# Two mixers' block inverses issued in step, a held-back order for small products, and low-rank products of split parts

## The chip, the cores and the metric

One core of one Trainium2 chip runs the whole kernel. The metric is device microseconds of one execution, the median over the runs shown. TensorE is PE in the rows, its weight loads are PEld, VectorE is DVE, ScalarE is ACT, GpSimd is POOL, SyncE (which issues most transfers) is SP.

## The reference

One layer of a hybrid encoder, 512 tokens of width 2048, all in fp32:

```
y  = RMSNorm(x) @ W_in                      # 59 column blocks of 128 in the kernel
h  = x + concat[GDN(y_gdn), RWKV7(y_rwkv)] @ W_out
h += CrossAttn(RMSNorm(h), RMSNorm(mem))    # 4 heads, 256 memory tokens
h += SquaredReLU-MLP(RMSNorm(h))
out = RMSNorm(h)
```

GDN is the gated delta rule (8 heads of 128), in chunks: with the decays `G`, `gamma = exp(G_i - G_j)` for `i >= j` and 0 elsewhere, and `M = strict_lower(kb k^T * gamma)`, it solves `(M + I) [U W] = rhs` and then scans over the chunks. RWKV-7 (16 heads of 64) is a token recurrence that the kernel also writes as chunks with a triangular inverse. Its decay and its in-context rate come from two products of rank 64: `tanh(w_lo) @ w2` and `a_lo @ a2`.

## The kernel before

The program has two parts. The second (from `vp`, the values of the cross attention, to the end of the MLP) is untouched. The first holds the input projection, both mixers and two products of the cross attention's weights, and is written by a small planner.

**The big stream.** `projections` issues, for each of 59 column blocks, 48 matmuls of 128x512 into `py`: each fp32 weight is split into a high and a low part in float32r (`whi`, `wlo`), and `xhi`, `xlo` likewise, and three products of parts stand for one fp32 product. After the 59 blocks come 16 blocks `kp` and then 32 pieces `kq` of the same kind.

**The mixers.** `rwkv(j)`, j = 0 to 7, does two RWKV heads at a time, `gdn(h)`, h = 0 to 7, one GDN head. Each eats some of the seven `py` blocks of its turn through four row buffers `ybuf`. Their products are small and mostly in plain fp32: 64x64 and 64x128 ones that use a quarter or a half of the array, and 128x64 and 128x128 ones that use all of it. Names as the rows show them: `pW`, `pA` are the two low-rank products of a turn (64 rows deep, 512 wide, on the lower and the upper half of the array). `ri..` and `gj..` are the products of the two levels that put the 16x16 inverses together (`inverse_levels` for GDN, the loop over `l` in `rwkv`); `gi..y`, `gi..z` finish a GDN inverse; `pu`, `pwt` apply the RWKV inverse. `rs` are the steps of the RWKV scan (128x64, 14 of them in a turn), `gs` those of the GDN scan (128x128, ten), each waiting for a VectorE step in between. `gn`, `pn`, `gon`, `pvr` are sums for norms, from `sumh`, `suml`.

**The 16x16 inverses.** `inverse_blocks` writes the triangular matrices to DRAM, reads the diagonal blocks back, solves them on GpSimd in 15 steps of a multiply and an add, and brings them back by DRAM (`bg16T`, `bg16U` for RWKV). For GDN the matrix is made from `E = exp(min(G_i - G_j, mask))`, which `mbias` makes zero on one side; GpSimd multiplies it by the constant `sneg` into `Es`, minus one strictly on the other side, and VectorE multiplies that with `pkk`.

**The planner.** Every mixer, the loader of weights and the big stream are generators that yield operations one at a time. `run` keeps the next operation of each, asks `start` when its engine and its operands would be free (from costs in `cost`, `CROSS` = 150 ns between engines), issues the one that could start first, and so fixes the order on every engine. `after(...)` holds a generator until an event, such as ("gi", h), the GDN head's diagonal inverses. For PE the key is

```
t = start(c[3])
key = (t + (0 if c[3][0] == "PE" else 150 * c[1]), c[1])
```

A RWKV turn is chained to the end of the levels of the one before; `gdn(h + 1)` is chained to the very end of `gdn(h)`. `kq` waits for "gated", the end of the last GDN head.

Of the kernel before, what the change touches and what calls it, by code (L numbers as in the profile page):

```python
# [17 lines left out]
P = 128  # L18
T = 512
# [8 lines left out]
for _n, _w in (("ident", 128), ("ones", 128), ("mA", 128),  # L28
               ("lv64", 2 * 64), ("cen", 64), ("sneg", 128), ("mbias", 128),
               ("rst64", 512)):  # L30
    CST[_n] = (_off, _w)
    _off += _w
# [13 lines left out]
def constants():  # L46
    c = np.zeros((P, NCST), np.float32)

    def put(name, a):
        o, w = CST[name]  # L50
        c[:, o:o + w] = a

    i = np.arange(P)
    put("ident", np.eye(P))
    put("ones", 1.0)
    j = np.arange(64)
    st = (j[:, None] < j[None, :]).astype(np.float32)
    inc = (j[:, None] <= j[None, :]).astype(np.float32)
    put("mA", np.tile(np.concatenate([st, inc], 1), (2, 1)))

    def level(n, s):
        a = np.arange(n)
        blk = a[:, None] // (2 * s) == a[None, :] // (2 * s)
        return (blk & (a[:, None] % (2 * s) >= s) & (a[None, :] % (2 * s) < s)).astype(np.float32)

    put("lv64", np.concatenate([np.tile(level(64, 16 << l), (2, 1)) for l in range(2)], 1))
    put("cen", np.tile(np.eye(64) - 1.0 / 64, (2, 1)))
    put("sneg", -(i[:, None] < i[None, :]).astype(np.float32))
    put("mbias", np.where(i[:, None] <= i[None, :], 1e30, -1e30))
    put("rst64", np.tile((np.arange(512) % 64 != 0).astype(np.float32), (P, 1)))  # L70
    return c


def build(tc, I, out):
# [109 lines left out]
    def cost(op):  # L184
        eng, nm, _, a, k, out, ins, _ = op
        n = out.free_size()
        if eng == "PE":
            l = ins[0]
            if l.dtype == F32R:
                return n * 0.417 + (13.3 if state["shape"] is None else 120.0)  # L190
            sh = (l.partition_size(), l.free_size())
            sw = 0 if state["shape"] == sh or sh == (128, 128) else 100
            if nm == "transpose":
                return sw + (110 if sh[0] > 64 else 40)
            if sh == (64, 64):
                return sw + (32 if op[5].tensor.name[:2] in ("ri", "pa", "pv", "pu", "pw", "pk", "gj") else 59)
            return sw + (115 if sh[0] < 128 and n == 128 else 2 * max(n * 0.84, 114))
# [15 lines left out]

    def start(op):
        eng, out = op[0], where(op[5])
        t, out_ = clock[eng], out
        for b, log in [(where(i), landed) for i in op[6]] + [(out, landed), (out, seen)]:
            x, by = log.get(b, (0.0, eng))
            if log is landed and b is out_ and eng == "SP" and by == "DMA":
                continue  # L220
            t = max(t, x + op[7][0] + (0.0 if by == eng else CROSS))
        return t
# [296 lines left out]
    def projections():  # L519
# [4 lines left out]
        for n in range(2, NIN):  # L524
            if n == NSQ[3] + 3:
                yield after("macc")
                pt = psb("pms", "mm", 2)
                mc = ybuf[macc[0]]
                yield TE.matmul(pt[:, 0:M], ones, mc[:, 0:M], start=True, stop=False)
                yield TE.matmul(pt[:, 0:M], ones, mc[:, M:2 * M], start=False, stop=True)  # L530
                chain(memnorm(pt, mc[:, M:2 * M]), 1)
            if n >= 4:
                yield after("py", n - 2)
            pt = psb(f"py{n}", "mm", 2)
            yield from gemm_([pt], xhi, xlo, 2 * n, left="x" if n == NIN - 1 else None)
            chain(evict(n, pt), 0)
# [20 lines left out]
        for i in range(2 * KD):  # L557
# [4 lines left out]
            if i == 0:  # L562
                yield after("gated")
            pts = [psb(f"kq{n}_{g}_{hh}", t, 2) for hh, t in enumerate(("mm", "mg"))]
# [45 lines left out]

    wa = pq.tile([P, T], F32, name="wa")
    sgh, sgl, sst = (pq.tile([P, T], F32R, name=n) for n in ("sgh", "sgl", "sst"))
# [3 lines left out]
    def rows():  # L616
# [9 lines left out]
        for c in range(4):  # L626
            yield DV.memset(rs128[g8, c * P:c * P + 1], 0.0)
        yield after("derived")
        yield from shiftmix(0, 0, wa)
        yield AC.activation(wa[0:64, :], wa[0:64, :], AF.Tanh)  # L630
        sg1, y2 = tl("gAq"), tl("gkt")
        yield from shiftmix(1, 1, sg1)
# [80 lines left out]

    def inverse_blocks(nm, store, m, tags, temps, ready, out, moved=False):

# [13 lines left out]
        for j in range(15):  # L729
# [3 lines left out]
                                   in1=Td[:, j:j + 1, 0:j + 1].broadcast_to([np_, w, j + 1]), op=ALU.mult)  # L733
            yield GS.tensor_tensor(out=Td[:, j + 1:16, 0:j + 1], in0=Td[:, j + 1:16, 0:j + 1], in1=t, op=ALU.add)
        Ud = D
# [18 lines left out]
    def inverse_levels(nm, Tm, Tt, NT, tags, mx, big):  # L754
# [4 lines left out]
        for l in range(2):  # L759
# [15 lines left out]
            rr = slice(0, P) if l == 0 else hA  # L775
            yield DV.tensor_tensor(out=Tm[rr, 0:2], in0=Tm[rr, 0:2], in1=d[rr, 4:6], op=ALU.add)
            yield DV.tensor_tensor(out=Tm[rr, 2:4], in0=Tm[rr, 2:4], in1=o[rr, 0:2], op=ALU.add)
            if l == 0:
                yield DV.tensor_tensor(out=Tt, in0=Tt, in1=d[:, 0:4], op=ALU.add)
                continue  # L780
            for r in (1, 0):
                w = slice(r * 64, r * 64 + 64)
                for c, h in ((slice(0, 2), HALF[r]), (slice(2, 4), HALF[1 - r])):
                    yield DV.tensor_tensor(out=big[HALF[r], c, w], in0=Tt[h, c], in1=d[h, c], op=ALU.add)


    def rwkv(j):
# [7 lines left out]
        pW, pA = psb(f"pW{j}"), psb(f"pA{j}")  # L795
        yield TE.matmul(pW, lw[0:64, :], wa[0:64, :], start=True, stop=True)
        yield TE.matmul(pA, lw[64:128, :], wa[64:128, :], start=True, stop=True)
        tw = short()
# [113 lines left out]
        for r in range(3):  # L912
            yield SL.dma_start(lg[r * 32:r * 32 + 32, P:2 * P], I["g2b"][:, js])
        yield after("ri", j)
        Tt = inv[1]
        Tm = inv[0]
# [38 lines left out]

        lgs = tile_of(pm, [P, 3 * P], F32R, "lgs", f"lgs{j}", 1)
        yield AC.copy(lgs[0:96, 0:2 * P], lg[0:96, :])
# [48 lines left out]
    def gdn(h):  # L1006
# [31 lines left out]
        yield after("zeros")  # L1038
        E, B = tl("gE"), tl("gqd")
        yield SL.dma_start(E, Rd[h:h + 1, :].broadcast_to([P, T]))  # L1040
# [10 lines left out]
        yield AC.activation(E, E, AF.Exp)  # L1051
        Es = tl("gEs")
        yield GS.tensor_tensor(out=c3(Es), in0=c3(E), in1=K("sneg").unsqueeze(1).broadcast_to([P, 4, P]), op=ALU.mult)
        kn = yield from normed(k_, None, "gkn", 0)
# [3 lines left out]
        for c in range(4):  # L1058
            cs = slice(c * P, (c + 1) * P)
            yield TE.matmul(pkk[:, cs], kn[:, cs], kb[:, cs], start=True, stop=True)  # L1060
        NTm = Es
        yield DV.tensor_tensor(out=NTm, in0=pkk, in1=Es, op=ALU.mult)

        def store(full):
# [4 lines left out]
        chain(inverse_blocks(f"gi{h}", store, 8, ("gkn", "gk", "gqn"), lambda: (tl("sgi"), tl("sgj", 240)),  # L1069
                             after("gq", h), inv, True), 1, ("gi", h))  # L1070
        q_ = yield from conv(1, 0, "gq")
# [26 lines left out]
        zt = gsh()  # L1098
        yield AC.activation(zt, z, AF.Tanh, scale=0.5)
        zs = tl("gz")  # L1100
        yield DV.scalar_tensor_tensor(out=zs, in0=zt, scalar=1.0, in1=z, op0=ALU.add, op1=ALU.mult)
        yfree.append(ys.pop(base + 3))
        yield after("gi", h)
        Tm, Tt = inv
        N3 = c3(NTm)
# [6 lines left out]
        Y = tl("gkn")  # L1112
        yield DV.tensor_copy(Y[hB, 0:256], p4[hB, 0:256])
        p5 = psb(f"gi{h}z", "mg")
# [3 lines left out]
        yield DV.tensor_copy(TtG[hA, :, 64:128], p5[hA, 0:256].rearrange("p (c t) -> p c t", t=64))  # L1118
        vns, Ss = tl("gE"), tl("gEG")
        for c in range(4):  # L1120
            cs = slice(c * P, (c + 1) * P)
            r1 = vb[:, cs]
            if c > 0:
                p1 = psb(f"gs1_{h}_{c}", "scg", 1)
                yield TE.matmul(p1[:, 0:P], wd[:, cs], Ss[:, cs], start=True, stop=True)
                r1 = short(P, "sg")
                yield DV.tensor_tensor(out=r1, in0=vb[:, cs], in1=p1[:, 0:P], op=ALU.subtract)
# [19 lines left out]
        o = tl("gkt")  # L1147
        yield AC.copy(o, po)
        sq = gsh()
        yield AC.activation(sq, o, AF.Square)  # L1150
# [5 lines left out]
        yield SL.dma_start(mixd[h], o)  # L1156
        if h < 7:
            chain(gdn(h + 1), 3)
        else:
            events.add(("gated",))  # L1160
# [870 lines left out]
```

## Time and profile before

| | us |
|---|---|
| runs before: median of 3 (lowest, highest) | 2897.46 (2896.79, 2902.83) |
| the profiled execution | 2898.35 |
| its span, first to last instruction | 2896.6 |
| PE busy in the span | 2870.5 |
| mean granted TensorE clock | 0.999 |

The profile is of one execution. Its span leaves out what lies around the program, 1.75 us. A matmul's row gives its start and a modelled end; since matmuls overlap, what a matmul costs is read from start to start. A plain fp32 matmul leaves two records, one of float32r one, a transpose one.

### The profile page before, as it was taken

How to read it: one execution, taken by the hardware profiler on the slowest of the kernel's cores; microseconds unless marked ns; L12 is line 12 of the kernel's file. 1: busy time of each engine (PE TensorE's matmuls, PEld its weight loads, DVE VectorE, ACT ScalarE, POOL GpSimd, SP SyncE). 2: the span in 40 equal slices, each digit the busy share in tenths (PEclk: the TensorE clock that was granted, in tenths of full speed). 3: DMA queues.
4: the chain of work that ended last, by engine and by line, in shares of the span. 5: the costliest groups of instructions: out<-in, count | busy, mean ns of one | idle time of the engine just before them, and what ended most of it. 6: DMA issues, size and time to landing. Idle time of an engine off the chain costs nothing.

```text
span 2896.6 us, 48156 instructions
## 1 busy us (share of the span) xinstructions
PE 2870.5 (99%) x18458; PEld 2408.6 (83%) x18458; DVE 2223.9 (77%) x3379; ACT 1561.9 (54%) x2256; POOL 310.2 (11%) x704
## 2 busy tenths in 40 slices
PE   9999999999999999999999999999999999999998
PEld 7787787887877888889888888888888878888887
DVE  7676676676676767769866898888998897878776
ACT  7544554554546555664455555555555655454444
POOL 0302213113113000001111100010010000000000
PEclk9999999999999999999999999999999999999999
DMA  5333333424334579797788767788777988776765
GB/s 193 100 89 85 99 90 86 105 69 100 105 98 137 159 243 298 267 308 199 205 218 209 195 194 219 229 234 248 214 206 207 288 261 278 221 261 209 255 191 178
DMA packets 304503, 546.64 MB, mean 189 GB/s; under 512 B 97224, under 2 KB 178380, under 8 KB 303248
## 3 DMA queue, kind: packets, MB, share of 16 engines
q1 hardware_dynamic: 245264, 449.17, 49.3%
q0 software_dynamic: 35840, 67.12, 11.6%
q10 hardware_dynamic: 23168, 27.27, 2.6%
q8 instruction: 145, 2.38, 0.3%
q14 instruction: 86, 0.70, 0.1%
HBM read 479.10 MB, written 131.48 MB: 211 GB/s over the span
## 4 chain that ended last, share of the span: by engine, by line
PE 92%; DVE 3%; DMA 2%; POOL 1%; issue 1%; ACT 1%; SPq 0%; ACTq 0%; POOLq 0%; DVEq 0%
PE py L228 20%; PE upx L1319 8%; PE upx L1321 4%; PE upy L1319 4%; PE dx L1786 4%; PE dx L1785 4%; PE dx L1788 4%; PE vp L122 3%; PE kq L228 3%; PE sc L122 3%; PE at L122 3%; PE kp L228 3%; PE vo L122 3%; PE upy L1321 2%; PE upz L1319 2%; PE opx L1319 2%
## 5 line engine op out<-in xcount | busy, mean ns | idle before, releaser
L130 ACT CAST whi<-ub 128x1024 fp32r<-128x1024 f32 x290 | 304.5, 1052 | 274.1 <-PE dy L1786 59.0
L131 DVE TENSOR_TENSOR wlo<-ub,whi 128x1024 fp32r<-128x1024 f32 x290 | 352.6, 1220 | 60.5 <-ACT whi L130 55.1
L228 PE MATMUL py<-xhi,whi 128*128 128x512 f32 x928 | 371.0, 400 | 6.3 <-ACT xhi L228 6.3
L228 PE MATMUL py<-xlo,whi 128*128 128x512 f32 x928 | 372.1, 401 | 0.0
L228 PE MATMUL py<-xhi,wlo 128*128 128x512 f32 x912 | 370.9, 407 | 0.0
L228 ACT CAST whi<-wraw 128x1024 fp32r<-128x1024 f32 (+1 forms) x180 | 187.3, 1041 | 260.9 <-PE py L228 162.1
L130 ACT CAST whi<-ua 128x1024 fp32r<-128x1024 f32 x205 | 215.5, 1051 | 191.3 <-PE dx L1786 62.3
L131 DVE TENSOR_TENSOR wlo<-ua,whi 128x1024 fp32r<-128x1024 f32 x205 | 249.7, 1220 | 52.6 <-ACT whi L130 51.8
L228 DVE TENSOR_TENSOR wlo<-wraw,whi 128x1024 fp32r<-128x1024 f32 (+1 forms) x178 | 223.2, 1254 | 70.5 <-ACT whi L228 68.1
L1319 PE MATMUL upx<-cb,whi 128*128 128x512 f32 x992 | 249.8, 394 | 0.7 <-DVE sl L1277 0.7
L228 PEld LDWEIGHTS py<-xhi,whi 128*128 128x128 f32 x928 | 175.3, 189 | 40.6 <-ACT xhi L228 6.6
L228 PEld LDWEIGHTS py<-xlo,whi 128*128 128x128 f32 x928 | 174.9, 189 | 38.3 <-DVE xlo L228 1.0
L1319 PEld LDWEIGHTS upx<-cb,whi 128*128 128x128 f32 x992 | 178.5, 189 | 33.0 <-DVE sl L1277 0.9
L228 PEld LDWEIGHTS py<-xhi,wlo 128*128 128x128 f32 x912 | 172.4, 189 | 32.7 <-issue 1.0
L1785 PE MATMUL dx<-whi,dh 128*128 128x512 f32 x480 | 186.7, 389 | 0.0
L1786 PE MATMUL dx<-whi,dl 128*128 128x512 f32 x480 | 186.7, 389 | 0.0
L1321 PEld LDWEIGHTS upx<-cb,wlo 128*128 128x128 f32 x992 | 135.3, 190 | 9.7
L1321 PE MATMUL upx<-cb,wlo 128*128 128x256 f32 x992 | 138.3, 282 | 0.0
L131 DVE TENSOR_TENSOR wlo<-wr,whi 128x1024 fp32r<-128x1024 f32 x80 | 97.7, 1223 | 43.5 <-ACT whi L130 42.4
L1788 PE MATMUL dx<-wlo,dh 128*128 128x512 f32 x480 | 128.6, 389 | 0.0
L228 ACT ACT_TABLE_LOAD x86 | 110.3, 1283 | 26.2 <-DVE suml_gn L228 11.6
L1319 PE MATMUL upy<-cb,whi 128*128 128x512 f32 x496 | 124.3, 392 | 0.0
(898 smaller groups left out, 6676.2 us busy)
## 6 DMA issues: line engine op xcount, KB each, us to landing
ws<-in_w_dn POOLq DMA_DIRECT2D x128, 512.0 KB, 7.2
wraw<-in_w_in SPq DMA_DIRECT2D x116, 512.0 KB, 3.8
ua<-in_w_dn SPq DMA_DIRECT2D x108, 512.0 KB, 4.5
ub<-in_w_up SPq DMA_DIRECT2D x71, 512.0 KB, 6.3
ua<-in_w_up SPq DMA_DIRECT2D x56, 512.0 KB, 4.7
ub<-in_w_dn SPq DMA_DIRECT2D x52, 512.0 KB, 4.7
sl<-cd SPq DMA_DIRECT2D x104, 256.0 KB, 5.0
ub<-ws SPq DMA_DIRECT2D x52, 512.0 KB, 4.2
```

Of the source, the lines that this page charges most:

```text
L122: PE.matmul(o, l, r, start=start, stop=stop)
L130: tie(S.copy(hi, src))
L131: V.tensor_tensor(out=lo, in0=src, in1=hi.bitcast(F32), op=ALU.subtract)
L228: f(*a, **k)
L1319: PE.matmul(pt, hi[:, k * P:k * P + P], parts[k], start=start and k == 0, stop=False, skip_group_check=True)
L1321: PE.matmul(pt[:, HA], lo[:, k * P:k * P + P], parts[k][:, HA], start=False, stop=k == 7, skip_group_check=True)
L1785: PE.matmul(pts[t], uh[:, x], hi[:, w], start=start and z == 0 and q == 0, stop=False, skip_group_check=True)
L1786: PE.matmul(pts[t], ul[:, x], hi[:, w], start=False, stop=False, skip_group_check=True)
L1788: PE.matmul(pts[t], uh[:, x], lo[:, w], start=False, stop=z == 1 and q == 3, skip_group_check=True)
```

## The change

Eight edits, all in the first part:

1. `sneg` and `Es` go. The GDN matrix is `pkk * E` with the other sign; the sign is taken back by `subtract` in place of `add` in `inverse_blocks`, `inverse_levels`, and by -1 in the copy `Y` (now a tensor_scalar).
2. `cost` charges a float32r matmul that follows a plain fp32 one of fewer than 128 rows 210 ns for the change of shape, not 120, and `run` adds `HOLD` = 150 ns to the start of a plain fp32 matmul that would follow a float32r one.
3. For j, h < 6 the RWKV levels wait for the GDN head to be as far ("gr"), and the GDN levels for the RWKV turn ("rr").
4. `wa` is split once into `wah`, `wal`, each turn's weights `lw` into `lws`; `pW` and `pA` become three float32r products each.
5. `gdn(h + 1)` is chained to the end of the head's inverse. Its tiles that were shared with the scan get buffers of their own (`gvn`, `gSs`, `gr`, `gqe`), and it waits for "gs" (the scan's products) and "ge" (the end) of the head before, ahead of q and of z.
6. `kq` waits for "solved", the last head's inverse, not for "gated".
7. The sums of the memory's norm wait for one `py` more.
8. A tile is renamed (`lgs`).

```
-    CROSS = 150.0
+    CROSS, HOLD = 150.0, 150.0
...
-                return n * 0.417 + (13.3 if state["shape"] is None else 120.0)
+                return n * 0.417 + (13.3 if state["shape"] is None else 120.0 if state["shape"][0] == P else 210.0)
...
                 t = start(c[3])
+                if c[3][0] == "PE" and state["shape"] is None and shape_of(c[3]) is not None:
+                    t = max(t, start(c[3], 0.0) + HOLD)
...
-                yield after("gated")
+                yield after("solved")
...
-    wa = pq.tile([P, T], F32, name="wa")
+    wah, wal = (pq.tile([P, T], F32R, name=n) for n in ("wah", "wal"))
...
+        yield from split_(wa, wah, wal)
...
-        yield TE.matmul(pW, lw[0:64, :], wa[0:64, :], start=True, stop=True)
-        yield TE.matmul(pA, lw[64:128, :], wa[64:128, :], start=True, stop=True)
+        lws = tile_of(pm, [P, 2 * P], F32R, "lws", f"lws{j}", 1)
+        yield from split_(lw, lws[:, 0:P], lws[:, P:2 * P])
+        for n, (l, r) in enumerate(((0, wah), (0, wal), (P, wah))):
+            for p_, h in ((pW, hA), (pA, hB)):
+                yield TE.matmul(p_, lws[h, l:l + P], r[h, :], start=n == 0, stop=n == 2)
...
         yield after("ri", j)
+        events.add(("rr", j))
+        if j < 6:
+            yield after("gr", j)
...
-        Es = tl("gEs")
-        yield GS.tensor_tensor(out=c3(Es), in0=c3(E), in1=K("sneg").unsqueeze(1).broadcast_to([P, 4, P]), op=ALU.mult)
...
-        NTm = Es
-        yield DV.tensor_tensor(out=NTm, in0=pkk, in1=Es, op=ALU.mult)
+        NTm = tl("gEs")
+        yield DV.tensor_tensor(out=NTm, in0=pkk, in1=E, op=ALU.mult)
...
+        if h:
+            yield after("gs", h - 1)
         q_ = yield from conv(1, 0, "gq")
...
+        if h:
+            yield after("ge", h - 1)
         zs = tl("gz")
...
         yield after("gi", h)
+        events.add(("gr", h))
+        if h < 6:
+            yield after("rr", h)
...
-        yield DV.tensor_copy(Y[hB, 0:256], p4[hB, 0:256])
+        yield DV.tensor_scalar(out=Y[hB, 0:256], in0=p4[hB, 0:256], scalar1=-1.0, scalar2=None, op0=ALU.mult)
...
-        vns, Ss = tl("gE"), tl("gEG")
+        if h < 7:
+            chain(gdn(h + 1), 3)
+        else:
+            events.add(("solved",))
+        vns, Ss = tl("gvn"), tl("gSs")
...
-        if h < 7:
-            chain(gdn(h + 1), 3)
-        else:
+        events.add(("ge", h))
+        if h == 7:
             events.add(("gated",))
```

What these edits do to the order shows in three places. The first is PE at the levels of turn 3 (`ri3` RWKV, `gj3` GDN, `po` and `pov` outputs of RWKV, `rs_3` its scan). Before:

```order
L228 MATMUL py_5417<-xhi_376,whi_5320 128x512
L228 MATMUL py_5417<-xlo_377,whi_5320 128x512
L228 MATMUL rs_3_6_5491<-BK_4862,BTz 128x64
L228 MATMUL py_5417<-xhi_376,wlo_5321 128x512
L228 MATMUL gj3u_5500<-gkn_5478,gqn_5390 64x64 x2
L228 MATMUL gj3t_5501<-gkn_5478,gqn_5390 64x64 x2
L228 MATMUL gj3u_5500<-gkn_5478,gqn_5390 64x64 x2
L228 MATMUL rs_3_7_5510<-Qs_4919,WTz 128x64
L228 MATMUL gj3t_5501<-gkn_5478,gqn_5390 64x64 x2
L228 MATMUL gj3u_5500<-gqn_5390,gkn_5478 64x64 x8
L228 MATMUL py_5417<-xhi_387,whi_5419 128x512
```

Now:

```order
L231 MATMUL ri3w_5420<-r_5044,GB_4737 64x64
L231 MATMUL gj3u_5433<-gkn_5341,gqn_5277 64x64 x2
L231 MATMUL gj3t_5434<-gkn_5341,gqn_5277 64x64 x2
L231 MATMUL gj3u_5433<-gkn_5341,gqn_5277 64x64 x2
L231 MATMUL gj3t_5434<-gkn_5341,gqn_5277 64x64 x2
L231 MATMUL gj3u_5433<-gqn_5277,gkn_5341 64x64 x8
L231 MATMUL py_5304<-xhi_377,wlo_5255 128x512
L231 MATMUL py_5304<-xhi_388,whi_5306 128x512
L231 MATMUL py_5304<-xlo_389,whi_5306 128x512
L231 MATMUL ri3u_5467<-E_289_5045,k_5418 64x64 x2
L231 MATMUL pov_5468<-GA_4736,BK_4964 64x64
```

The GDN levels stood in the RWKV scan and were cut by its steps; now they stand between the RWKV levels, with no `py` between the two. The second place is PE at the low-rank products of turn 3 (`pW`, `pA`) and what is around them. Before:

```order
L228 MATMUL py_3978<-xhi_398,whi_3980 128x512
L228 MATMUL rs_2_1_4100<-BK_3631,BTz 128x64
L228 MATMUL pW_4050<-wa,lw_4048 128x512
L228 MATMUL pA_4051<-wa,lw_4048 128x512
L228 MATMUL rs_2_2_4111<-Qs_3688,WTz 128x64
L228 MATMUL py_3978<-xlo_399,whi_3980 128x512
L228 MATMUL pqk_4118<-gqn_4068,gkn_3777 128x128 x4
```

Now:

```order
L231 MATMUL gi2y<-gk_3981,gEs_3808 64x64 x3
L231 MATMUL pW_4301<-wah,lws_4303 128x512
L231 MATMUL pA_4302<-wah,lws_4303 128x512
L231 MATMUL rs_2_2_4359<-BK_3695,BTz 128x64
L231 MATMUL gi2z<-TtG,gkn_4356 64x64 x4
L231 MATMUL pW_4301<-wal,lws_4303 128x512
L231 MATMUL rs_2_3_4371<-Qs_3761,WTz 128x64
L231 MATMUL pA_4302<-wal,lws_4303 128x512
L231 MATMUL gs_2_0_4376<-gv_4031,TtG 128x128
L231 MATMUL pW_4301<-wah,lws_4303 128x512
L231 MATMUL rs_2_3_4385<-BK_3695,BTz 128x64
L231 MATMUL pA_4302<-wah,lws_4303 128x512
```

The two products became six, cut apart by steps of both scans, which now run side by side. The third place is GpSimd after the RWKV inverses of turn 2 (`sr`) and ahead of those of GDN head 2 (`sgi`). Before:

```order
L228 TENSOR_TENSOR sr_3474<-sr_3474,sr_3475 64x15
L228 COPY sr_3474<-sr_3474 64x256
L228 TENSOR_TENSOR gEs_3598<-gE_3460,cst 128x512
L228 MEMSET sgi_3863 32x256
L228 MEMSET sgi_3863 32x16
```

Now:

```order
L231 TENSOR_TENSOR sr_3512<-sr_3512,sr_3513 64x15
L231 COPY sr_3512<-sr_3512 64x256
L231 MEMSET sgi_3824 32x256
L231 MEMSET sgi_3824 32x16
L231 TENSOR_TENSOR sgj_3825<-sgi_3824 32x15
```

The mask's multiply is gone in all eight heads; the rest of GpSimd's list is the same.

## Rows read from the trace of the kernel before

**Rows 1.** The page: the chain that ended last, shares of the span by engine.

```profile
PE 92%; DVE 3%; DMA 2%; POOL 1%; issue 1%; ACT 1%; SPq 0%; ACTq 0%; POOLq 0%; DVEq 0%
```

**Rows 2.** Busy us by stretch, split where `vp` begins: PE, PEld, DVE, ACT, POOL, clock.

```profile
0.00:1125.00 1125.00, 1110.91 (x9403) 903.82 (x9404) 776.49 (x1407) 617.75 (x881) 202.08 (x547) 1.00 0.43 123
1125.00:2896.60 1771.60, 1759.56 (x9057) 1504.79 (x9055) 1447.43 (x1973) 944.14 (x1376) 108.08 (x157) 1.00 0.77 231
```

**Rows 3.** Who PE waited for, 0 to 1125 us: total, times, longest.

```profile
PE gn L228 <- DVE suml_gn L228: 2.6, 3, 0.9
PE ri6x L228 <- DMA r<-bg16T: 1.6, 2, 1.4
PE pu L228 <- ACT whi L228: 1.3, 1, 1.3
PE ri0t L228 <- DMA E<-bg16U: 0.6, 1, 0.6
```

**Rows 4.** Timeline of PE around one 64x64 stretch (`pu`, `pwt`): start, us.

```profile
358.69 0.39 PE L228 MATMUL py<-xhi,wlo 128*128 128x512 f32 x1
359.00 0.27 PE L228 MATMUL pu<-tA,E 64*64 64x64 f32 x2
...
359.11 0.22 PE L228 MATMUL pu<-tA,E 64*64 64x64 f32 x2
...
359.17 0.23 PE L228 MATMUL pu<-tA,E 64*64 64x64 f32 x2
...
360.10 0.50 PE L228 MATMUL py<-xhi,whi 128*128 128x512 f32 x1
360.44 0.40 PE L228 MATMUL py<-xlo,whi 128*128 128x512 f32 x1
```

**Rows 5.** Timeline of PE around one lone scan step.

```profile
365.02 0.40 PE L228 MATMUL py<-xlo,whi 128*128 128x512 f32 x1
365.26 0.33 PE L228 MATMUL rs<-BK,BTz 128*128 128x64 f32 x2
365.40 0.48 PE L228 MATMUL py<-xhi,wlo 128*128 128x512 f32 x1
365.72 0.39 PE L228 MATMUL py<-xhi,whi 128*128 128x512 f32 x1
```

**Rows 6.** Timeline of PE around the low-rank products of turn 3.

```profile
367.54 0.33 PE L228 MATMUL rs<-BK,BTz 128*128 128x64 f32 x2
367.80 0.69 PE L228 MATMUL pW<-wa,lw 64*128 64x512 f32 x1
367.81 0.69 PE L228 MATMUL pA<-wa,lw 64*128 64x512 f32 x1
...
368.93 0.43 PE L228 MATMUL rs<-Qs,WTz 128*128 128x64 f32 x2
369.17 0.48 PE L228 MATMUL py<-xlo,whi 128*128 128x512 f32 x1
369.49 0.50 PE L228 MATMUL pqk<-gqn,gkn 128*128 128x128 f32 x3
```

**Rows 7.** The mask on GpSimd, a weight split on VectorE, the wait on PE.

```profile
L228 DVE TENSOR_TENSOR wlo<-wraw,whi x178: 684/1225/2756, 10.0 to 1120.5; 128x1024 fp32r<-128x1024 f32 x176, 128x512 fp32r<-128x512 f32 x2
...
223.48 2.75 DVE L228 TENSOR_TENSOR wlo<-wraw,whi 128x1024 fp32r<-128x1024 f32 x1 [1.80 <-ACT whi L228]
...
223.84 1.30 POOL L228 TENSOR_TENSOR gEs<-gE,cst 128x512 f32<-128x512 f32 x1
...
226.88 0.50 PE L228 MATMUL gn<-suml_gn,onesr 128*128 128x512 f32 x1 [0.88 <-DVE suml_gn L228]
```

**Rows 8.** Timeline of the end of one GDN inverse.

```profile
394.88 0.67 PE L228 MATMUL gi2y<-gk,gEs 64*64 64x64 f32 x8
...
396.74 0.43 DVE L228 COPY gkn<-gi2y 64x256 f32<-64x256 f32 x1
...
397.52 0.68 PE L228 MATMUL gi2z<-TtG,gkn 64*64 64x64 f32 x8
```

More of the change, by code (lines that the diff above doesn't have):

```diff
@@ L28 @@
 for _n, _w in (("ident", 128), ("ones", 128), ("mA", 128),
-               ("lv64", 2 * 64), ("cen", 64), ("sneg", 128), ("mbias", 128),
+               ("lv64", 2 * 64), ("cen", 64), ("mbias", 128),
                ("rst64", 512)):
@@ L67, in constants @@
     put("cen", np.tile(np.eye(64) - 1.0 / 64, (2, 1)))
-    put("sneg", -(i[:, None] < i[None, :]).astype(np.float32))
     put("mbias", np.where(i[:, None] <= i[None, :], 1e30, -1e30))
@@ L212, in cost, with shape_of, start @@
         return 100.0
-    def start(op):
+    def shape_of(op):
+        l = op[6][0]
+        return None if l.dtype == F32R else (l.partition_size(), l.free_size())
+    def start(op, t=None):
         eng, out = op[0], where(op[5])
-        t, out_ = clock[eng], out
+        t, out_ = clock[eng] if t is None else t, out
         for b, log in [(where(i), landed) for i in op[6]] + [(out, landed), (out, seen)]:
@@ L526, in projections @@
                 yield after("macc")
+                yield after("py", n - 1)
                 pt = psb("pms", "mm", 2)
@@ L628, in rows @@
         yield after("derived")
+        wa = tl("gqd")
         yield from shiftmix(0, 0, wa)
         yield AC.activation(wa[0:64, :], wa[0:64, :], AF.Tanh)
+        yield from split_(wa, wah, wal)
         sg1, y2 = tl("gAq"), tl("gkt")
@@ L712, in views, with inverse_blocks @@
         return full, blk
-    def inverse_blocks(nm, store, m, tags, temps, ready, out, moved=False):
+    def inverse_blocks(nm, store, m, tags, temps, ready, out, moved=False, op=ALU.add):
         np_ = 4 * m
@@ L733, in inverse_blocks @@
                                    in1=Td[:, j:j + 1, 0:j + 1].broadcast_to([np_, w, j + 1]), op=ALU.mult)
-            yield GS.tensor_tensor(out=Td[:, j + 1:16, 0:j + 1], in0=Td[:, j + 1:16, 0:j + 1], in1=t, op=ALU.add)
+            yield GS.tensor_tensor(out=Td[:, j + 1:16, 0:j + 1], in0=Td[:, j + 1:16, 0:j + 1], in1=t, op=op)
         Ud = D
@@ L775, in inverse_levels @@
             rr = slice(0, P) if l == 0 else hA
-            yield DV.tensor_tensor(out=Tm[rr, 0:2], in0=Tm[rr, 0:2], in1=d[rr, 4:6], op=ALU.add)
-            yield DV.tensor_tensor(out=Tm[rr, 2:4], in0=Tm[rr, 2:4], in1=o[rr, 0:2], op=ALU.add)
+            yield DV.tensor_tensor(out=Tm[rr, 0:2], in0=Tm[rr, 0:2], in1=d[rr, 4:6], op=ALU.subtract)
+            yield DV.tensor_tensor(out=Tm[rr, 2:4], in0=Tm[rr, 2:4], in1=o[rr, 0:2], op=ALU.subtract)
             if l == 0:
-                yield DV.tensor_tensor(out=Tt, in0=Tt, in1=d[:, 0:4], op=ALU.add)
+                yield DV.tensor_tensor(out=Tt, in0=Tt, in1=d[:, 0:4], op=ALU.subtract)
                 continue
@@ L783, in inverse_levels @@
                 for c, h in ((slice(0, 2), HALF[r]), (slice(2, 4), HALF[1 - r])):
-                    yield DV.tensor_tensor(out=big[HALF[r], c, w], in0=Tt[h, c], in1=d[h, c], op=ALU.add)
+                    yield DV.tensor_tensor(out=big[HALF[r], c, w], in0=Tt[h, c], in1=d[h, c], op=ALU.subtract)
     def rwkv(j):
@@ L954, in rwkv @@
             chain(rwkv(j + 1), 3)
-        lgs = tile_of(pm, [P, 3 * P], F32R, "lgs", f"lgs{j}", 1)
+        lgs = tile_of(pm, [P, 3 * P], F32R, "lgs", f"lg_s{j}", 1)
         yield AC.copy(lgs[0:96, 0:2 * P], lg[0:96, :])
@@ L1038, in gdn @@
         yield after("zeros")
-        E, B = tl("gE"), tl("gqd")
+        E, B = tl("gE"), tl(("gqd", "gqe")[h % 2])
         yield SL.dma_start(E, Rd[h:h + 1, :].broadcast_to([P, T]))
@@ L1069, in gdn @@
         chain(inverse_blocks(f"gi{h}", store, 8, ("gkn", "gk", "gqn"), lambda: (tl("sgi"), tl("sgj", 240)),
-                             after("gq", h), inv, True), 1, ("gi", h))
+                             after("gq", h), inv, True, ALU.subtract), 1, ("gi", h))
+        if h:
+            yield after("gs", h - 1)
         q_ = yield from conv(1, 0, "gq")
@@ L1125, in gdn @@
                 yield TE.matmul(p1[:, 0:P], wd[:, cs], Ss[:, cs], start=True, stop=True)
-                r1 = short(P, "sg")
+                r1 = tl("gr", P, 2)
                 yield DV.tensor_tensor(out=r1, in0=vb[:, cs], in1=p1[:, 0:P], op=ALU.subtract)
@@ L1146, in gdn @@
                 yield TE.matmul(po[:, cs], Ss[:, cs], qd[:, cs], start=False, stop=True)
-        o = tl("gkt")
+        events.add(("gs", h))
+        o = tl("gSs")
         yield AC.copy(o, po)
-        sq = gsh()
+        sq = tl("gvn")
         yield AC.activation(sq, o, AF.Square)
```

## The prediction

> **What bounds the kernel now.** The chain that ended last is PE for 92% of the span [rows 1]; read it first, since it says that an edit pays only if it takes time from PE or lets PE wait less. [...] The second part, 1771.6 us, is untouched, and I carry it over. Third, who PE waited for in the first part [rows 3]: the four longest, leaving the start aside, are 6.1 us in all. So the mixers are hidden beside the big stream, and what they cost is the time their own small products hold PE. That is read from start to start around a stretch of them [rows 4 to 6]; a big float32r matmul takes 0.23 to 0.24 us so measured (365.02 to 365.26).
>
> Times are summed against the profiled execution, 2898.35 us (span 2896.6 and 1.75 around it). The median of the runs shown is 0.9 us lower, and I subtract the sum from that median. A measurement of this kernel tells about 0.2%, 5.8 us, from no change.
>
> **The change, part by part.**
>
> *Levels in step, held-back products (edits 2, 3, 5).* No product is added; they are regrouped. A stretch of 64x64 products costs more than its products: from the last `py` before `pu` to the second one after it are 1.75 us (358.69 to 360.44), of which two big matmuls are 0.47; the thirty products go in fifteen rounds of 0.06 (359.11 to 359.17), 0.9; so entering and leaving cost 0.4 [rows 4]. In the built order PE goes from full-size products into 64x64 ones 111 times before and 96 times after. 15 x 0.4 = 6.0 us less. I use the whole price, since a stretch that vanishes takes both ends with it.
>
> The scan steps: before, 69 `rs` and 80 `gs` stood alone between big matmuls; now 43 and 29 do, and 50 times an `rs` stands right before a `gs`. A lone `rs` costs 0.70 - 0.47 = 0.23 [rows 5]. What a pair saves no row shows. Bounds: nothing, and half a lone `rs`, 0.12, as it streams half the columns that a `gs` does: 0 to 6.0 us. An `rs` behind `pA` moved the next start by 0.24 [rows 6], as a lone one does, so I stay near nothing: 1.5.
>
> *Low-rank products (edit 4).* Before, a pair takes 1.13 us (367.80 to 368.93), and `rs` ahead of it is 0.12 longer than a lone one's 0.14 (0.26 against 365.26 to 365.40) [rows 5, 6]: 1.25 each, eight times, 10.0 us. After, there are 48 products. In the order 17 of them stand alone, and there are 8 twos, one three and two sixes, 28 stretches in all, where there were 9; 12 of the 28 begin right behind 64x64 products. Occupancy: the two halves start 0.01 apart in the fp32 pair (367.80, 367.81), so two neighbours on different halves may take one slot of 0.23: 33 slots, 7.6 us; if they never do, 48 slots, 11.0. Entering and leaving a half-array stretch: 0.12 by the pair's own row, 0.4 by the 64x64 row, halved for the 12: 2.6 to 8.8. Together 10.2 to 19.8, against 10.0. The pair's row has the same shape, so I stay near the low end: 1.0 us more. [...]
>
> The new splits are nine casts on ScalarE and nine subtractions on VectorE, eight of 128 columns or 256 and one of 512. Each is below the 1.2 us of a 1024-wide one [rows 7], so under 11 us per engine over 1125, with VectorE idle 348 and ScalarE 507 [rows 2]: nothing, unless one stands just ahead of a step PE waits for.
>
> *No mask (edit 1).* Removes eight GpSimd multiplies of 1.30 us. They are on no chain by themselves, but look at 223.84: while one runs, a weight split on VectorE that lasts 1.2 us in the median takes 2.75, the next sum is late, and PE's `gn` stands still for 0.88 [rows 7]. The wait list has three such waits, 2.6 us in all [rows 3]; with the multiply away I take all three as gone. What is late next there is the table load that follows on ScalarE, and nothing on PE hangs on it. Subtract for add and a scaled copy for a copy cost the same.
>
> *Waits for transfers.* The RWKV levels of turns 0 to 5 now wait for GDN, and so stand later (`ri3x` 137 big matmuls later in the order), while their diagonal blocks come back from DRAM no later: `ri0t`'s 0.6 goes [rows 3]. `ri6x`'s 1.6 and `pu`'s 1.3 may stay: turns 6 and 7 are not in step.
>
> *What the added waits hold up.* They are the planner's, so on PE big matmuls pass. Behind the held RWKV levels are `pu`, the scan, and next turn's `pW`, whose rows of `py` sit in four buffers. In the order `pn4` stands 48 big matmuls later, one block; then three buffers are taken and the fourth is free, so the stream goes on. At the end the last GDN norm stands 62 big matmuls later but still some 44 ahead of `kq`, so `kp` still covers it. "Solved" for "gated", and the wait ahead of the memory's sums, cost and give nothing: no `kq` is in the wait list. On SyncE the next head's two row broadcasts move up past a few weight loads, with buffers freed earlier. Yet steps of two scans now share VectorE, and some gaps shrink: between `gi..y` and `gi..z` were 2.64 us (394.88 to 397.52), of which the copy is 0.43 [rows 8]; in the order there are now about three matmuls. I add 1.0 us of new waits, over bounds of 0 and the 21.6 below.
>
> Sum: -6.0 - 1.5 + 1.0 - 2.6 - 0.6 + 1.0 = -8.7. 2897.5 - 8.7 = **2888.8 us**; the profiled execution would be near 2889.7.
>
> **Rivals.**
>
> *More than that.* Pairs save 6.0, the low-rank part costs 0.2, `ri6x` and `pu` stop waiting (2.9), no new wait: -6.0 - 6.0 + 0.2 - 2.6 - 0.6 - 2.9 = -17.9, 2879.6. For it: every such piece is the end of a bound. Against: all at once.
>
> *The scattered low-rank products eat it.* 9.8 for that part, nothing from pairs: -6.0 + 9.8 - 2.6 - 0.6 + 1.0 = +1.6, 2899.1. For it: most of the 48 stand alone between steps of full size, where a big matmul would have stood free. Against: the small price in the pair's own row. [...]
>
> *Slower: gaps too short for VectorE.* A hop as in rows 8 needs a product's end, a copy of 0.43 and its turn behind evictions and weight splits, up to 1.2 us. If three hops in each turn (`gi..y` to `gi..z`, on to `gs`, level to level) make PE stand for 0.9 us, that is 2.7 x 8 = 21.6 in place of 1.0: +11.9, 2909.4. It decides from (8.7 + 1.0 + 5.8) / 8 = 1.9 us per turn on. Against: no VectorE step of the scans or levels is among the longest waits now [rows 3], and the planner does count the copies.
>
> *The change does not do it.* The order excludes most of that: levels do stand together, the mask is gone. What it can't show is whether waits fall elsewhere; that is in the chances.
>
> **How the numbers follow.** My forecast, with the rival above it, ends faster by over 5.8 us: 0.65 (0.53 and 0.12). Within 5.8 us: the low-rank rival and half-way cases, 0.26. Slower: the hops, 0.09. The range: down to just under the rival with more, 2878, up past the low-rank rival by some 3 us, 2902; the long waits are left out above.
>
> **What would show it.** In the new profile, waits of `gn` for `suml` gone; no `gEs` on GpSimd, and no weight split over 2 us beside it; the first part shorter by 9 us and the second the same; `pW` and `pA` rows at about 0.23 from start to start when side by side; waits for DMA on `ri0` to `ri5` gone. Wrong if PE's wait list names `gi..z`, `gs` or `rs` behind VectorE for more than 2 us in all, if `py` waits for an eviction, or if a low-rank stretch costs over 0.4 us beyond its slots.

## The result and the profile after

| | before | after |
|---|---|---|
| median of the runs beside each other | 2898.44 us (4 runs) | 2913.14 us (4 runs) |
| ratio, 95% interval | | 1.005 [1.0036, 1.0064] |
| span of the profiled execution | 2896.6 us | 2909.2 us |
| first part, to the first `vp` | 1125.0 us | 1140.4 us |

The change is 14.7 us slower, where 8.7 us less was forecast; 2913 lies above the range. Read first the table by stretch, as in [rows 2] (columns: stretch, its length, busy us with counts of PE, PEld, DVE, ACT and POOL, granted clock, share and GB/s of the DMA engines):

```profile
0.00:1140.40 1140.40, 1122.93 (x9419) 921.34 (x9420) 774.68 (x1416) 617.26 (x889) 201.29 (x539) 0.99 0.42 121
1140.40:2909.20 1768.80, 1758.93 (x9058) 1504.83 (x9056) 1448.05 (x1973) 944.31 (x1376) 108.08 (x157) 1.00 0.78 231
```

All of the loss, 15.4 us, is in the edited part; the second part is 2.8 us shorter. And the granted clock of the first part is no longer 1.00. (Over whole executions it is 0.993 or 0.994 in all four of the change and 0.999 in all of the kernel before, so it is not one unlucky execution.) The list of PE's waits there, beside [rows 3]:

```profile
PE py L231 <- ACT xhi L231: 7.9, 1, 7.9
PE gj5x L231 <- DMA gk<-bg8T: 2.8, 2, 2.5
PE gj2x L231 <- DMA gk<-bg8T: 1.9, 2, 1.1
PE ri6x L231 <- DMA r<-bg16T: 1.5, 2, 1.2
PE kp L231 <- DVE wlo L231: 1.3, 2, 1.0
PE gj6x L231 <- DMA gk<-bg8T: 1.0, 2, 0.6
```

`gn` and `ri0t` are gone, as forecast, and so is `pu`; `gj` (the GDN levels) now waits for its own diagonal blocks. Leaving the start aside, the whole list has 9.4 us, the one of before 7.2. So waits explain 2.2 us, and the start, which waits 7.9 us here for its first split and 6.3 before, another 1.6 (no cause is shown; it is 6.3 to 7.9 in the profiles of the experiments too). The rest stands in the same table over short stretches: one ahead of a fall of the clock, four with a fall, at the low-rank products of turns 1, 3, 4 and 7, and two (630, 744) at the same place in turns 5 and 6:

```profile
160.00:164.50 4.50, 4.50 (x30) 3.01 (x30) 2.26 (x8) 0.00 (x0) 0.00 (x0) 1.00 0.02 4
164.50:171.70 7.20, 7.20 (x24) 5.84 (x24) 4.16 (x9) 4.07 (x6) 0.00 (x0) 0.53 0.00 0
396.00:403.60 7.60, 7.60 (x24) 5.19 (x23) 3.14 (x11) 1.37 (x2) 0.00 (x0) 0.55 0.05 15
519.00:526.60 7.60, 7.60 (x25) 5.93 (x25) 3.82 (x11) 3.34 (x5) 0.00 (x0) 0.55 0.00 1
630.00:637.00 7.00, 7.00 (x43) 5.44 (x43) 4.50 (x15) 2.96 (x4) 0.00 (x0) 1.00 0.46 96
744.00:751.00 7.00, 7.00 (x43) 5.45 (x43) 4.54 (x15) 3.00 (x5) 0.00 (x0) 1.00 0.33 92
847.40:857.60 10.20, 10.20 (x67) 7.27 (x66) 4.38 (x13) 2.09 (x3) 0.00 (x0) 0.50 0.21 65
```

In four places the granted clock is down at 0.50 (where the row has 0.53 or 0.55, the stretch taken reaches a little past it). What was lost is length times one less the clock: 3.4 + 3.4 + 3.4 + 5.1 = **15.3 us**, an estimate that takes all of PE's work there to go at half speed. PE is busy for the whole of each, so no view of waits shows any of it. The timeline of PE around the first of them (start, busy us) shows what it did before:

```profile
159.60 0.39 PE L231 MATMUL py<-xhi,whi 128*128 128x512 f32 x1
...
160.17 0.43 PE L231 MATMUL rs<-Qs,WTz 128*128 128x64 f32 x2
...
161.02 0.49 PE L231 MATMUL pW<-wah,lws 64*128 64x512 f32 x1
161.03 0.49 PE L231 MATMUL pA<-wah,lws 64*128 64x512 f32 x1
161.45 0.43 PE L231 MATMUL rs<-BK,BTz 128*128 128x64 f32 x2
...
162.42 0.49 PE L231 MATMUL pW<-wal,lws 64*128 64x512 f32 x1
162.84 0.43 PE L231 MATMUL rs<-Qs,WTz 128*128 128x64 f32 x2
163.20 0.49 PE L231 MATMUL pA<-wal,lws 64*128 64x512 f32 x1
163.62 0.49 PE L231 MATMUL gs<-gv,TtG 128*128 128x128 f32 x2
...
164.47 0.50 PE L231 MATMUL rs<-BK,BTz 128*128 128x64 f32 x2
...
166.07 0.77 PE L231 MATMUL py<-xlo,whi 128*128 128x512 f32 x1
...
170.48 0.63 PE L231 MATMUL py<-xlo,whi 128*128 128x512 f32 x1
170.91 0.63 PE L231 MATMUL py<-xhi,wlo 128*128 128x512 f32 x1
...
171.66 0.39 PE L231 MATMUL py<-xlo,whi 128*128 128x512 f32 x1
171.88 0.39 PE L231 MATMUL py<-xhi,wlo 128*128 128x512 f32 x1
```

From 159.60 to 166.07, 6.47 us, no full-size product (128x128 weights, 512 columns) comes: half-array low-rank products alternate with steps of both scans and 64x64 products. The clock falls at 164.7, 5.1 us after the last full-size one began. In turns 5 and 6 the like stretch lasts 5.1 us, and no fall follows. With the clock down, a `py` takes 0.43 us (170.48 to 170.91), and 0.22 once the clock is back. The same rows price a scattered product at the full clock: 0.42 for a lone one (162.42 to 162.84), where its slot is 0.23, and 0.43 for a pair (161.02 to 161.45).

So two theories went into the experiments. **Theory 1**: stretches without a full-size product bring the clock down, and the scattered low-rank products make them. **Theory 2**: new waits, of `gj` for transfers and of scan steps for VectorE, are the cause.

### The profile page after: what moved, and what is told of

It is laid out like the page before. It is cut to its first block, busy times and chain, and to the rows that moved or that the text cites. A ratio compares the mean times of both kernels' runs of the same rounds, so it can differ in the third digit from the quotient of the medians.

```text
span 2909.2 us, 48164 instructions
## 1 busy us (share of the span) xinstructions
PE 2881.9 (99%) x18474; PEld 2426.2 (83%) x18474; DVE 2222.7 (76%) x3388; ACT 1561.6 (54%) x2265; POOL 309.4 (11%) x696
## 4 chain that ended last, share of the span: by engine, by line
PE 95%; DMA 1%; DVE 1%; ACT 1%; POOL 0%; issue 0%; SPq 0%; ACTq 0%; DVEq 0%; POOLq 0%
PE py L231 22%; PE upx L1342 8%; PE upx L1344 4%; PE upy L1342 4%; PE dx L1808 4%; PE dx L1811 4%; PE dx L1809 4%; PE kq L231 3%; PE vp L121 3%; PE at L121 3%; PE vo L121 3%; PE sc L121 3%; PE kp L231 3%; PE upy L1344 2%; PE upz L1342 2%; PE dy L1808 2%
```

## The experiments

Each run is compared with the kernel before on the same chip (2896.8 to 2898.2 us); ratios are to that, with a 95% interval.

**Undoing the low-rank edit.**

```
-   for n, (l, r) in enumerate(((0, wah), (0, wal), (P, wah))):
...
+   TE.matmul(pW, lw[0:64, :], wa[0:64, :], ...); TE.matmul(pA, lw[64:128, :], wa[64:128, :], ...)
```

> The change with edit 4 undone: pW and pA of each turn are again one fp32 product each, adjacent; levels in step, held-back products and the rest stay. [...] Theory 2 (the time went into new waits: gj for DMA, some 5.7 us, and the scan steps' short hops to VectorE; the lower clock only follows from TensorE standing still more): those waits stay, the clock still falls in some turns, and at most 4 us come back: 2909 to 2914.

2901.7 us, 1.0015 [1.0006, 1.0024]: 11.4 us below the change, near the 15.3 that theory 1 has for the clock and more than theory 2 allows; but the clock still fell, to 0.50 for 3.4 us each, at two new places (columns as above):

```profile
260.00:266.60 6.60, 5.14 (x121) 3.69 (x121) 2.98 (x8) 1.04 (x1) 0.00 (x0) 1.00 0.27 51
266.60:270.00 3.40, 3.32 (x48) 2.72 (x37) 2.31 (x6) 0.00 (x0) 0.00 (x0) 0.50 0.83 237
```

Ahead of the first stand the levels of both inverses, 64x64 products with few full-size ones between, and a wait of `gj1x` of 1.4 us: no low-rank product is needed. The second (727.4) follows 3.77 us without a full-size product; four like stretches of this run, at 276.6, 388.8, 500.3 and 612.0, led to none, and nor did a longer one, of 4.54 us at 161.5. So length alone does not decide; what else does is open. And one order does not bring the same falls each time: the eleven executions of this kernel have mean clocks from 0.996 (2906.6 and 2907.0 us) to 0.999 (2899.0 and 2899.2). The order also parts the fp32 pair in seven turns, where the kernel before does in one. At 723.77 `pW` takes 1.05 to the next start, and `pA` behind an `rs` 1.06, where a pair took 1.13 [rows 6]. By an estimate, 1.0 us a pair, that is 6 us for the six turns more, so the time of this run is no clean measure of either theory.

**The low-rank edit alone, and as one group.** The second run takes the kernel before and edit 4; the third and fourth issue the six products of a turn without anything between, in the change and in the kernel before.

```
-   yield TE.matmul(p_, lws[h, l:l + P], r[h, :], ...)
+   yield [TE.matmul(p_, lws[h, l:l + P], r[h, :], ...) for ... ]
```

> The kernel before with edit 4 alone (low-rank products of high and low parts, 48 half-array products in place of 16 fp32 ones). In its order these stand in twos, threes and sixes, four of them alone. Theory 1: a product scattered singly among scan steps is what brings the clock down, so here the clock stays at 1.00 throughout the first part, and the time is the kernel before's plus 0 to 6 us (my term was +1.0 with ends of +0.2 and +9.8). Theory 2 makes no other forecast of the clock, but would have the low-rank part cost at the upper end, +6 to +10. If the clock falls here too, half-array products of the new form are enough by themselves.

2900.0 us, 1.0008 [0.9999, 1.0017]: +2.9, inside the range for the time, but the clock did not stay up: there is one fall of 3.4 us (810.3), and 3.9 us of waits of `ri4x` and `ri6x`. That fall follows 64x64 products among which PE stood 1.1 us, not a low-rank product; the low-rank stretches of this run, up to 4.2 us without a full-size product, led to none.

> The change with the six low-rank products of a turn issued as one unbroken group (all else as in the change). Theory 1: no falls of the clock in the first part, mean granted clock 0.999, time 2890 to 2899, below the change by 14 to 23 (15 from the clock, the rest from fewer entries into half-array stretches: 8 in place of 28). Theory 2: the waits for DMA and VectorE stay and the time is 2906 to 2914.

**2881.4 us, 0.9951 [0.9938, 0.9963]**: faster than either kernel, 31.8 us below the change, 8.6 below what I expected. Its first part in the table by stretch, and its list of waits:

```profile
0.00:1108.60 1108.60, 1098.72 (x9419) 906.66 (x9419) 775.64 (x1416) 616.79 (x889) 202.51 (x539) 1.00 0.44 125
```

```profile
PE py L231 <- ACT xhi L231: 6.5, 1, 6.5
PE kp L231 <- DVE wlo L231: 2.0, 3, 1.1
PE gj7w L231 <- DVE gv L231: 0.8, 1, 0.8
PE pvr L231 <- DVE suml_pvr L231: 0.4, 1, 0.4
```

The count of PE's instructions is that of the change, 9419. No fall, no wait for a transfer. Of the 31.8 us the clock is 15.3, the waits 6.2 and the start 1.4, by the rows; the other 8.9 are PE's own time for its products. The group by itself, in turn 0:

```profile
56.05 0.39 PE L231 MATMUL py<-xlo,whi 128*128 128x512 f32 x1
56.37 0.49 PE L231 MATMUL pW<-wah,lws 64*128 64x512 f32 x1
56.38 0.49 PE L231 MATMUL pA<-wah,lws 64*128 64x512 f32 x1
56.71 0.39 PE L231 MATMUL pW<-wal,lws 64*128 64x512 f32 x1
...
56.94 0.39 PE L231 MATMUL pW<-wah,lws 64*128 64x512 f32 x1
...
57.27 0.50 PE L231 MATMUL py<-xhi,wlo 128*128 128x512 f32 x1
```

From `py` to `py` 1.22, less one slot of 0.23: 0.99 us for six. The halves start 0.01 apart, a pair takes one slot (56.71 to 56.94), and in and out cost 0.3 together.

> The kernel before with edit 4 alone, the six low-rank products of a turn issued as one unbroken group. A lone group of six measured 0.99 us (from the first start to the next full-size product, less one slot) and 1.17 with two scan products in it, an fp32 pair with four scan products 1.65 to 1.75; six or seven turns times 0.3 to 0.5: -2 to -4 us, 2893 to 2896, no fall of the clock. If the group is worth nothing and only the falls counted, 2896 to 2899.

2888.0 us, 0.9970 [0.9959, 0.9981]: -9.2, more than expected. Grouping, with the order that it brings, is thus worth 12 us beside the same edit ungrouped; some 5 of them are waits and 1.7 the fall that the other order had.

**Without the levels in step.** The two lines `yield after("gr", j)` and `yield after("rr", h)` are taken out; the low-rank products then stand in sixes in seven turns.

> The change without edit 3: the levels of the two inverses no longer wait for one another; the low-rank products then stand in sixes in seven of eight turns, with no scan step between them. Theory 1: the clock stays at 1.00, since no half-array product stands alone; the 64x64 entries return (115 for 96, +6 to +8 us by my price), mask and waits stay gained: 2896 to 2904, mean granted clock 0.999. Theory 2: the waits of gj for DMA (5.7 us) go, and only they and the hops come back: 2903 to 2910, with the clock where it was in some turns.

2887.3 us, 0.9964 [0.9951, 0.9978], no fall: below both ranges, as the grouped kernel was below its own. It is 6.0 us above the grouped kernel with levels in step, with 3.0 us of waits for its 3.2. PE goes into 64x64 products 115 times, in the grouped kernel 101 times; at the 0.4 of [rows 4] that is 5.6. So where the products stand together, edit 3 gains 6.0.

**A limit on stretches of small products.** The rule in words, with times of the planner's own costs:

```
+   if not big(op) and small > 2000 ns: take a full-size product that can start within 200 ns
```

> The change whole, its low-rank products still scattered, with one rule added to the planner: when it has issued 2 us of small products by its own costs since the last full-size one, and a full-size one can start within 0.2 us, that goes first. Theory 1, as the first four runs leave it (the clock falls behind a long stretch in which no full-size product comes, 6.5 to 7.6 us long in the change, whatever the small products are): no such stretch is over 3.5 us, no fall of the clock in the first part, mean granted clock 0.999, time 2890 to 2898. Rival (the scattered half-array products themselves bring the clock down, however the stretch is cut): falls stay in turns 1, 3, 4 and 7, and the time is 2906 to 2914.

2899.2 us, 1.0007 [0.9998, 1.0016], 1.2 above the expected range, 14 below the change. None of the four falls is left, though the products are nearly as scattered (25 stretches for 28; turn 7 has its six together, so it tests nothing there). Two others came, of 6.8 and 3.4 us, each behind a `gj` that stood waiting for its blocks (2.7 us ahead of the first, at 375.2, and 3.0 ahead of the second, shown here), so falls come behind theory 2's waits as well:

```profile
715.00:719.90 4.90, 1.67 (x51) 1.06 (x49) 0.94 (x3) 0.00 (x0) 0.00 (x0) 1.00 0.17 35
719.90:723.30 3.40, 3.40 (x55) 2.46 (x49) 2.01 (x4) 1.05 (x1) 0.00 (x0) 0.50 0.55 145
```

**The low-rank products made full-size.** Two weight tiles, each with 64 rows of zeros, so that every product contracts over 128 rows.

```
-   TE.matmul(p_, lws[h, l:l + P], r[h, :], ...)
+   TE.matmul(p_, lws[u][:, l:l + P], r, ...)
```

> The change, with each low-rank product made full-size: its weights stand in a tile whose other 64 rows are zero, so that it contracts over 128 rows, with the same result. The 48 products stay scattered among the scan steps; in the built order turns 1 and 7 read as in the change (where the clock fell), the others nearly so. Theory 1 (the clock falls where no full-size product comes for long): these now count as full-size, so no fall in turns 1 and 7 nor elsewhere in the scans, some 15 us back from the clock, 4 from half-array products that cost more than their slots, and +3 for 48 slots of 0.23 in place of 33: 2894 to 2902, with the waits for transfers left as they are. Rival (the scan steps' scatter and their waits bring the clock down, whatever the low-rank products are): falls in turns 1 and 7 as in the change, 2905 to 2914.

2894.1 us, 0.9989 [0.998, 0.9998]; no fall at the low-rank products of any turn. Those of turns 1 and 7, in the change's order, stand in these two stretches:

```profile
158.00:171.50 13.50, 13.50 (x86) 11.54 (x85) 10.30 (x32) 4.03 (x6) 0.00 (x0) 1.00 0.23 58
830.50:838.00 7.50, 7.50 (x82) 6.17 (x81) 6.99 (x21) 2.15 (x4) 0.00 (x0) 1.00 0.24 79
```

In turn 1 the scan steps, and their hops, are those of the change, which has no wait there either; only the low-rank products differ. That rules theory 2 out for this fall; ahead of those of turns 3 and 4 the change's own rows have no wait. Turn 7 decides nothing: in the change PE stood 1.0 us for `gj6x` among its low-rank products, and here it did not. The same products of turn 1, from an `rs` to a `py` and each once in both runs, also price the fall:

```profile
159.61 0.43 PE L231 MATMUL rs<-Qs,WTz 128*128 128x64 f32 x2
...
163.14 0.33 PE L231 MATMUL rs<-BK,BTz 128*128 128x64 f32 x2
...
166.79 0.39 PE L231 MATMUL py<-xlo,whi 128*128 128x512 f32 x1
```

From 163.14 to 166.79 are 3.65 us; in the change they take 7.19 (164.47 to 171.66): 3.5 for one fall that the count by the clock puts at 3.4. Ahead of it, from `rs` to `rs`, the change takes 4.30 us (160.17 to 164.47) and this run 3.53, though no two of its low-rank products share a slot. Two other falls came (487.9, 713.1), again behind `gj` waiting for its blocks.

**Single edits of the kernel before, and holding back taken out.** The mask's edit alone; the holding back and its costs alone; the change, and the grouped change, without the two lines that use `HOLD`; the mask's edit with grouped products.

> The kernel before with edit 1 alone (no mask multiply on GpSimd, signs moved into subtracts). By my term -2.6 us (the three waits of gn): 2893 to 2896 beside 2897.1; gn gone from TensorE's wait list. If the waits only move to another step, 2896 to 2899. No fall of the clock in either case.

2890.3 us, 0.9977 [0.9968, 0.9986]: -6.9, below both ranges. `gn` left the list, but so did `ri6x` and `pu`, which no mask bears on: the order was rebuilt.

> The kernel before with edit 2 alone (small products held back by 150 ns behind full-size ones, and the planner's price of entering a half-array product). By itself it regroups little (111 entries into 64x64 products as before, 84 lone rs for 69, six of the fp32 products alone in place of two), so my reading that edits 2 and 3 together gave -7.5 us puts nearly all of it on edit 3: 2895 to 2900 here. If it is worth something by itself, 2890 to 2894.

2905.1 us, 1.0027 [1.0016, 1.0037]: **+7.9**, both cases missed. Its profile has 3.4 us of waits of `ri6x`, 1.2 of `ri2x`, a fall of 3.4 us behind the former, and six fp32 products parted from their pairs, for two in the kernel before.

> The six low-rank products as one group (as in e3_lowrank_six) and the holding back taken out again. If parts add up, holding back costs 7.9 us here too: 2881.4 - 7.9 = 2873.5, say 2871 to 2877. If its cost in e7_hold_alone was only the waits for transfers that its order ran into (ri6x, ri2x, ri5x, kp), which e3_lowrank_six does not have, then nothing comes back: 2880 to 2884. No fall of the clock in either case, since no stretch without a full-size product is longer than in e4_no_step.

2904.0 us, 1.0024 [1.0015, 1.0033], both cases missed: 22.6 above the grouped kernel, with two falls of 6.8 us, the longer wait ahead of them being:

```profile
598.94 0.44 PE L231 MATMUL gj4x<-gk,gEs 64*64 64x64 f32 x2 [4.07 <-DMA gk<-bg8T]
```

Why the blocks are late is on SyncE's queue (start, us): first this run, whose `pkk`, the product that the blocks come from, starts at 565.44; then the grouped kernel, whose `pkk` starts at 555.64.

```profile
567.37 1.28 SPq L231 DMA_DIRECT2D r<-bg16T  x2
568.75 2.55 SPq L231 DMA_DIRECT2D E<-bg16U  x4
...
572.05 1.25 SPq L231 DMA_DIRECT2D ndgi<-gEs  x2
576.66 0.34 SPq L231 DMA_DIRECT2D sgi<-ndgi  x1
```

```profile
552.55 1.28 SPq L231 DMA_DIRECT2D r<-bg16T  x2
553.93 2.55 SPq L231 DMA_DIRECT2D E<-bg16U  x4
...
557.87 1.25 SPq L231 DMA_DIRECT2D ndgi<-gEs  x2
561.93 0.34 SPq L231 DMA_DIRECT2D sgi<-ndgi  x1
```

`pkk` to GpSimd's load (`sgi`) is 11.2 us in the one and 6.3 in the other: in the one, the store `ndgi` stands behind the RWKV blocks on their way back (its matrix is ready at 567.9), in the other those have just gone. In the change's turn 5 the same six transfers stand between store and load: 692.64 to 699.99, 7.4 us in place of 4.1.

> The change without the holding back; low-rank products scattered as in the change, and long stretches of small products in turns 2, 3 and others in the built order. If the falls of the clock are what counts, they stay, and the time is 2903 to 2914. If holding back were what brings them about, they go, and it is 2890 to 2898.

2922.3 us, 1.0086 [1.0073, 1.01]: nine falls in the first part, 4.0 us of waits of `ri7x`, 3.4 of `gj2x`. Four falls come at low-rank products (turns 1, 3, 4 and 6), five behind a wait of 2.0 to 4.0 us, one of these an `rs` that stood 2.3 us for VectorE. The falls stay, as theory 1 has it, but the time is above the range, and here holding back helps, by some 9 us; the falls cost 24 us by the same count, 8.5 more than in the change.

> The kernel before with edit 1 and the low-rank products in one group of six, nothing else. Adding up e6_mask_alone (-6.9) and e8_six_alone (-9.2): 2881, say 2878 to 2884, no fall of the clock. If both gains are in part the same waits (gn, ri6x, pu went in both), 2885 to 2888.

2892.5 us, 0.9985 [0.9976, 0.9993]: the gains do not add up, and neither case held. With the group, the mask's edit is 4.6 us slower than without it. The lists of waits do not show why (4.9 us in all, against 4.5; `ri6x` 1.9, against 0.5); PE goes into 64x64 products 118 times, against 108, which at 0.4 is 4.0.

## Why the prediction was wrong

**The clock: the step that failed.** Every product was priced as if the granted clock were the 1.00 of [rows 2] throughout. No term and no rival had it fall. It cost 15.3 us by the rows; without that the change would stand near 2898, inside the range, though not at the forecast. The first part came out 24.1 us above its forecast (+15.4 for -8.7): 15.3 the clock, 4.4 waits (+2.2 for -2.2), 1.6 the start, 2.8 PE's own products (-3.7 for -6.5).

The cap and the full-size products, which part or replace what stands ahead of the falls, leave none of the four. They bring back 14 and 19 us of time, not all of it the clock, since each has two other falls, of 5.1 us by the same count. The mean clock is 0.996 to 0.999 in the 22 executions of the two, where the change has 0.993 or 0.994. So it is shown for turns 1, 3 and 4 that a stretch without full-size products, in which low-rank products and scan steps alternate, stands at each fall, and that no fall comes where it is parted or its products are full-size. For turn 7, with a wait among its products, it is argued. What decides is open: of like stretches some were followed by a fall and some not (turns 5 and 6; those of the first experiment; stretches of the change in which `gj` waited 1.9 and 2.8 us, with no fall behind them).

Nor does idle time of PE stand ahead of every fall. PE stood 4.07 us ahead of one behind `gj` (the grouped change without `HOLD`, 598.94), but in the change it was busy 4.50 of 4.50 us ahead of the falls of turns 1 and 3 (160.0 to 164.5, 392.3 to 396.8) and 4.60 of 4.60 ahead of turn 4's (515.0 to 519.6).

**Low-rank products (+1.0): mis-sized.** Pairs share a slot, as the lower bound had it (0.01 apart, 0.23 a pair); but a lone one costs 0.19 over its slot and a pair 0.20, where the 11.0 us that I chose left 0.12 for each of the 28 stretches. By the change's own rows 17 lone and 8 pairs at 0.42, a three at some 0.65 (an estimate, between a pair and a six) and two sixes at 0.99 are 13.1 us, +3.1 against the 10.0, before the shape changes that they force on their neighbours. The price I chose, near the low end because fp32 pairs had the same shape, was for a group. It also counted the way in alone: the `rs` behind `pA` and its `py` take 0.56 (368.93 to 369.49), not 0.46 as at a lone `rs`, so by [rows 5, 6] the way out costs another 0.10. What the 0.19 us of a lone product over its slot goes into, no row shows.

**Levels in step (-6.0): right, where nothing else breaks; scan pairs (-1.5): nothing.** The grouped kernel with and without edit 3 differ by 6.0. A pair, which no row showed before, now has its rows: in the change an `rs`, a `gs` and their `py` take 0.68 (406.57 to 407.25), less a slot 0.45, and a lone `rs` and a lone `gs` take 0.23 each. So the lower bound held and the 1.5 was not there. In the change the terms are inside the rest: 15.4 - 15.3 (clock) - 2.2 (waits) - 1.6 (start) = -3.7 for levels, scan pairs and low-rank products, where -6.5 was forecast; with +3.1 for the low-rank products and nothing for pairs, the levels are left with -6.8.

**Holding back: taken as part of the -7.5, not shown.** Alone it cost 7.9, and there I had priced regrouping only, not the fp32 pairs that it parts nor the waits for blocks. Taken out of the change it cost 9.2, and out of the grouped change 22.6, most of it waits and falls. So it can gain or lose by the order around it, and no run gives its share.

**Mask (-2.6): the waits of `gn` went in every kernel that has the edit**, the change among them; but they shrank to 0.8 us in two kernels without it as well, so they hang on the order too. The edit alone gave -6.9 and on top of the group +4.6; so a rebuilt order moves several us either way, and a term of 2.6 is not read from totals.

**Waits for transfers (-0.6) and added waits (+1.0).** `ri0t` went, `ri6x` stayed (1.5). That the "diagonal blocks come back from DRAM no later" holds for RWKV; it missed that GDN's blocks then queue with RWKV's on SyncE. The change has 5.7 us of `gj`, and three of the experiments two falls each behind it. The queue is read for turn 5 of the change and for one wait of an experiment; that it is the same in the others is taken, not shown. The rival on short hops has no support in the change: no scan step is in its list of waits, and the fall of turn 1 vanished with the hops in place.

**What was seen rightly**: the second part unchanged within 3 us, `gn` gone, halves in one slot, the scaled copy at the price of a copy (`gkn<-gi..y`, 427 ns beside 428) and the subtract near that of the add (`sgi` on GpSimd, median 288 ns beside 295). None of my own signs of being wrong came up: at the full clock a lone low-rank product is 0.19 us over its slot, where I had set 0.4, and the list of waits names no `gi..z`, `gs` or `rs`. They were all about waits and prices; none looked at the clock.

The grouped change, at 2881.4, comes nearest to what the prediction described (-15.7 where it said -8.7): its levels in step and its mask without the falls and late blocks. What the grouping itself gives was in no term.

## What to carry to other kernels

Where small products fill the gaps of a stream, look at the granted clock of short stretches, not of the part, and at that of every execution: here three falls of 6.8 us stood behind no wait, and the engine looked busy in them (in the first 7.20 of 7.20 us at 0.53). Try half-array products as one group, pairs on different halves side by side: here six took 0.99 us, where a lone one took 0.42. Try full-size products between long runs of small ones: here the cap left none of the change's four falls, though two others came behind waits. After each edit that rebuilds an order, test it with the others in place: here one edit was worth -6.9 and +4.6, another +7.9 and -22.6.

## What was not expected of the hardware

TensorE's granted clock fell to 0.50 while the profile has the engine busy without a gap (4.50 of 4.50 us, then 7.20 of 7.20 at 0.53), for 6.8 us at a time and once 10.2. With the low-rank products over 128 rows, half of them zero, it did not: turn 1 in the same order kept 1.00 from 158 to 171.5 us. Scattered, these padded products were also the cheaper ones, 3.53 us against 4.30 from `rs` to `rs` at the full clock. Two fp32 half-array products cost 1.13 us together [rows 6] and 1.05 each apart.
